# One-hot compares for four tokens at once, scaled on ScalarE, and 48 instead of 72 tiles of U ahead, in a transformer layer with single-neuron experts

## The chip, the cores and the metric

The kernel runs on one core of a Trainium2 chip. The metric is the device time of one execution in microseconds (us), lower is better. TensorE does the matrix products, VectorE and ScalarE work on the elements, GpSimd issues the gathers, and SyncE and ScalarE issue most of the transfers between the chip's memory and the on-chip memory.

## The reference

One layer for 512 latent tokens of width 2048, with 256 tokens of context: a modulated norm, a mixing half (pooling beside differential attention), then a half of experts, then a last norm. The change lies in the experts' half. For every token, two halves of a query score 128 keys each; the best 16 of each side are combined, and the 16 best pairs of eight heads name 128 experts out of 128 x 128, each with a gate. Then

```python
u = peer_u[eidx]                                   # (token, head, 16, 2048)
act = gelu(einsum('thkd,td->thk', u, hb))
v = peer_v[eidx]
out = einsum('thkd,thk->td', v, gate * act)
```

All of it is float32.

## The kernel before

**Two ways for the experts.** The first 128 tokens gather the rows of `peer_u` and `peer_v` that they picked (`slots`): 128 gathers of U and 128 of V, each a row of 2048 per token, each followed by one pass of VectorE (lines 676 and 687). The other 384 tokens (`TD`) take all 16384 experts densely, in 128 tiles of 128 experts: `u_tile` multiplies a tile of U with the tokens and applies the gelu, the result is multiplied with the gates (zero for experts that a token didn't pick), and the products with V sum it up. Float32 factors are split into a high and a low part, a cast on ScalarE and a subtraction on VectorE (`split`, lines 112 and 113; `weights` does it for what comes from memory, with three buffers of each half tile), and three products stand for one. A tile of U has 48 products (line 709).

**Gates.** `decode` makes, from a token's picks, the first key's number, the second key's and the gate; `pick` transposes these into `pT`, so that each token is a column. `combine` then makes the 128 x 128 table of gates of one token as a product of two one-hot matrices: L has a one where the first key's number is the column's, R has the gate where the second key's is. L is one compare on VectorE (line 751), R a compare with a multiplication in the same instruction (line 752), each of 128 x 128, with ten buffers each (`LRB`). Four tokens, a group here, share one buffer of `pg` in PSUM, which ScalarE copies into `ge` (line 754); `pg` has two buffers. After eight groups, 32 tokens, the 2 MB of `ge` go to `g_s` in the chip's memory (line 757); `ge` has one buffer.

**Stages.** The gates need the decoded picks, and V's products need the gates. So 72 tiles of U (`SPILL`) run ahead: their results go to `sg_s` in memory (`spill`). Five tiles (`PRE`) come first, then `combine` is advanced behind each tile until its 96 groups are made, two tiles (`GEND`) before the end:

```python
for n in range(todo):
    spill(1)
    if n in late:
        pick(late[n])
    if n >= GS:
        pump(GRATE)
    while made < 8 * (TD // 32) * (n + 1) / (todo - GEND):
        made += 1
        next(steps, None)
```

`pump` starts the gathers that are due, `GRATE` for a tile. Then come 16 chunks of eight tiles (`CH`) in the order 72 to 127, 0 to 71: for a tile from 72 on U is computed in the chunk, for the others the spilled result is read back (`sg`); then four column blocks of V's products (line 841, 288 products a chunk) with `pump` between them at `RATE`. Seven chunks have U in them, nine do not.

**What sets the order.** The order of instructions on each engine is fixed when the program is built: a scheduler goes through the instructions in program order and lets a later one go first where, by its planned costs, an earlier one would still wait. On the chip each engine takes its instructions in that order, and waits by semaphores.

Of the kernel before, what the change touches and what calls it, by code (L numbers as in the profile page):

```python
# [10 lines left out]
F32 = mybir.dt.float32  # L11
# [4 lines left out]
AF = mybir.ActivationFunctionType  # L16
OP = mybir.AluOpType
# [6 lines left out]
T = 512  # L24
# [7 lines left out]
TOPK = 16  # L32
TD = 384

# the first two sections of the modulation: k-tiles that go to the tensor engine whole (the others
# split in two), the steps after which a block of tokens is normalized, buffers
SEC0 = (3, 7, 11, 15)
SEC1 = (0, 1, 2, 3, 4, 5)
BLK = (0, 2, 3, 5, 7, 9)
AWB = 7  # L40
AHB = 2

# attention, in steps of a projection's k-tile (48 a head): how long the products of zc are held back,
# a head's first block of scores and the next ones (QKL: the last head's), from scores to transposed
# probabilities and on to the values, the operands of the next head's keys, pooling's last product
LEAD = 3
QK0 = 8
QKD = 4
QKL = 6
# [5 lines left out]
ADA_REST = 4  # L55
POOLS = (3, 2, 1, 0)

# experts: tiles of U ahead of V, tiles a chunk, tiles before the gates are combined and the end
# that is left free, when tokens' picks are decoded, rows gathered a tile
SPILL = 72  # L60
CH = 8
PRE = 5
LATE = ((8, 0), (12, 2), (30, 3))
GS = 9
GEND = 2
GRATE = 1.15
LRB = 10
RATE = (256 - (SPILL - PRE - GS) * GRATE) / (2 * NKEY - SPILL - 11)


def body(tc, xin, ctx, vecs, lamv, ada1, ada2, adab2, n2g, fing, win, poolw, wout, wq, keys,
         ut, u, v, rope, icnt, out):
    nc = tc.nc
    V, S, G, E = nc.vector, nc.scalar, nc.gpsimd, nc.tensor

    with ExitStack() as whole:
# [18 lines left out]
        ones = const.tile([128, 1], F32, name="ones")  # L95
        iota = const.tile([128, 128], F32, name="iota")
# [27 lines left out]
            V.tensor_scalar(tmp, ss, 1.0 / n, EPS, op0=OP.mult, op1=OP.add)  # L124
            G.tensor_tensor(dst, tmp, nhalf[:, 0:dst.shape[-1]], OP.pow)

# [1 line left out]
        # h^T without its shift; the shift's columns (latent, context) stand beside it as two  # L128
        # more tokens, and what they project to is added to every token's projection.
        # columns: shifts 0:2, context 2:258, shifts 258:260, latent 260:772  # L130
        hstack = ExitStack()
        hp = pool(hstack, "hp", side="right")
        h_hi = hp.tile([128, KT, HW], F32R, name="h_hi")
# [12 lines left out]
        S.copy(cols, svp[:, 0:89])  # L146
        S.activation(scol.rearrange("p j k -> p (j k)"), cols[:, 0:32], AF.Silu)
        V.tensor_scalar(g08, cols[:, 88:89], 0.8, None, op0=OP.mult)
        # silu(c), silu(c_ctx): whole (beside two columns of zeros), and split in two
        sc4 = a1.tile([128, KT, 4], F32, name="sc4")  # L150
        sr4 = a1.tile([128, KT, 4], F32R, name="sr4")
        V.memset(sc4, 0.0)
        V.tensor_copy(sc4[:, :, 0:2], scol.rearrange("p j k -> p k j"))
        split(sr4[:, :, 0:2], sr4[:, :, 2:4], sc4[:, :, 0:2])

        # normalized tokens, transposed in place: [feature, block, k-tile, token]
        xall = a0.tile([128, 6, D], F32, name="xall")

        def norm_block(b):
# [75 lines left out]
            split(h_hi[:, :, c0:c0 + 2], h_lo[:, :, c0:c0 + 2], sh)  # L235
        a1stack.close()

# [1 line left out]
        with ExitStack() as st:  # L239
            at = pool(st, "at")  # L240
            ps = pool(st, "psA", 1, PSUM)
# [14 lines left out]
                V.tensor_add(dst, dst, zs[:, 0:n])  # L256

            def project(idx, zl, zc):
                # one step a k-tile; zc's first products are held back for LEAD steps
                late = []  # L260
                for half in range(2):
                    hi, lo = weights(win[idx, :, half * 8:(half + 1) * 8, :], [128, 8, 128])
                    for k8 in range(8):
                        k = half * 8 + k8

                        def mm(part, k=k, k8=k8, hi=hi, lo=lo):
                            for p, (x, y) in enumerate(((hi, h_hi), (hi, h_lo), (lo, h_hi))):
                                E.matmul(part[0], x[:, k8, :], y[:, k, part[1]], start=k == 0 and p == 0, stop=k == KT - 1 and p == 2)  # L268
                        mm(zl)
                        late.append(mm)  # L270
                        if k >= LEAD - 1:
                            for m in late:
                                m(zc)
                            late = []
                        if k < KT - 1:
                            yield
# [22 lines left out]
                agenda.setdefault(n, []).append(fn)  # L299

            def k_operands(h):
                # stacked for the products: [k_hi; k_hi] of each map, and k_lo
                d = heads[h]
                kr = d["kr"]
                d["kk"] = kk = at.tile([128, 2, TK], F32R, name="kk")
                d["k_lo"] = k_lo = at.tile([128, TK], F32R, name="k_lo")
                for m, a, b in HALVES:
                    S.copy(kk[a, m, :], kr[a])
                    nc.scalar.dma_start(kk[b, m, :].bitcast(F32), kk[a, m, :].bitcast(F32))
                    V.tensor_sub(k_lo[a], kr[a], kk[a, m, :].bitcast(F32))  # L310
# [121 lines left out]
                    G.dma_start(m_s[:, sec * 512:(sec + 1) * 512], b)  # L432

            def pooling(g):
                # the window's mean minus the token itself
                ic = at.tile([128, T], F32, name="aw", bufs=3)
                nc.scalar.dma_start(ic, icnt[g:g + 1, :].to_broadcast([128, T]))
                zl, zc = psums()
                yield from project(36 + g, (zl[:, 0:256], slice(516, HW)), (zc, slice(258, 516)))
                sb = shift_of(zc)  # L440
                za = at.tile([128, T + 16], F32, name="kr", bufs=2)
                zb = at.tile([128, T + 16], F32, name="aw", bufs=3)
                V.memset(za[:, 0:8], 0.0)
                V.memset(za[:, T + 8:T + 16], 0.0)
                S.activation(za[:, 8:264], zc[:, 2:258], AF.Identity, bias=sb[:, 0:1])
                S.activation(za[:, 264:T + 8], zl[:, 0:256], AF.Identity, bias=sb[:, 0:1])
                n, src, w = T + 16, za, 1
                while w < 2 << g:
                    n -= w
                    V.tensor_add(zb[:, 0:n], src[:, 0:n], src[:, w:w + n])  # L450
                    src, w = zb, 2 * w
                V.tensor_mul(ic, zb[:, 8 - w // 2:8 - w // 2 + T], ic)
                V.tensor_sub(ic, ic, za[:, 8:T + 8])
                pw = at.tile([128, 128], F32, name="on", bufs=2)
                nc.scalar.dma_start(pw, poolw[g])

                def mix():
                    pt = ps.tile([128, T], F32, name="T", bufs=2)
                    E.matmul(pt, pw, ic, start=True, stop=True)
                    yo = at.tile([128, T], F32, name="aacc")  # L460
                    V.tensor_scalar(yo, pt, cols[:, 80 + g:81 + g], cols[:, 84 + g:85 + g], op0=OP.add, op1=OP.mult)
                    G.dma_start(o_s[g], yo)
                at_step(48 * H + 16 * POOLS.index(g) + 16 + MIX, mix)
                yield

            for h in range(H):
# [4 lines left out]
                for qp in range(2):  # L471
                    t = units[4 * qp + 3] + PT0
# [14 lines left out]
            steps, ada, owed_ada, n = fill(), ada_steps(), 0.0, 0  # L487
            while agenda or steps is not None:
                if steps is not None and next(steps, 0) == 0:
                    steps = None  # L490
# [9 lines left out]
        pstack.close()  # L500
        hstack.close()

# [1 line left out]
        f0p = pool(whole, "f0p")  # L504
        f0 = f0p.tile([128, D], F32, name="f0")
        xstack = ExitStack()
# [5 lines left out]
        with ExitStack() as st:  # L512
            op = pool(st, "op", side="right")
# [62 lines left out]
            nc.sync.dma_start(f_lo.bitcast(F32), fq_lo[:, :, 128:T].bitcast(F32))  # L576
        xstack.close()

# [1 line left out]
        ub = pool(whole, "ub")  # L580
        psU = pool(whole, "psU", 1, PSUM)
        rtstack = ExitStack()
# [5 lines left out]
        with ExitStack() as st:  # L588
# [12 lines left out]

            for hp in range(16):
                pq = ps.tile([128, T], F32, name="pq", bufs=2)
                # the first product begins with the tokens that are ready first
                ws = []
                for cs in ((slice(0, 256), slice(256, T)) if hp == 0 else (slice(0, T),)):
                    for half in range(2):
# [52 lines left out]
            V.reciprocal(sm, sm)  # L660
            V.tensor_tensor(g3, g3, sm[:, :, None].to_broadcast([128, PH, 16]), op=OP.mult)

# [1 line left out]
        acc0 = gp.tile([128, D], F32, name="acc0")  # L664
        vw = v.rearrange("(a b) d -> a b d", b=NKEY)

# [54 lines left out]
        with ExitStack() as st:  # L721
# [16 lines left out]
                S.copy(picks[b], pt)  # L738

            def combine():  # L740
                # gates by token and expert: one one-hot product a token
                for tt in range(TD // 32):
                    ge = gb.tile([128, 128, 32], F32, name="ge", bufs=1)
                    pT = picks[1 + tt // 4]
                    for t4 in range(0, 32, 4):
                        pg = ps.tile([128, 4, 128], F32, name="pg", bufs=2)
                        for i in range(4):
                            t = (tt % 4) * 32 + t4 + i
                            L = gb.tile([128, 128], F32, name="L", bufs=LRB)
                            R = gb.tile([128, 128], F32, name="R", bufs=LRB)  # L750
                            V.tensor_scalar(L, iota, pT[:, 0, t:t + 1], None, op0=OP.is_equal)
                            V.tensor_scalar(R, iota, pT[:, 1, t:t + 1], pT[:, 2, t:t + 1], op0=OP.is_equal, op1=OP.mult)
                            E.matmul(pg[:, i, :], L, R, start=True, stop=True)  # L753
                        S.copy(ge[:, :, t4:t4 + 4].rearrange("p b t -> p t b"), pg)
                        if t4 < 28:
                            yield
                    nc.scalar.dma_start(g_s[tt], ge)
                    yield
# [177 lines left out]
```

## Time and profile before

| | |
|---|---|
| median of 3 runs | 3678.8 us (3674.42 to 3694.43) |
| profiled execution, first to last instruction | 3665.6 us; the runs' times hold what lies around the span too, and the median is 13.2 us above it |
| busy: TensorE, VectorE, ScalarE, GpSimd | 3533.5, 2669.5, 1391.0, 463.5 us |
| granted share of TensorE's full clock over the span | 0.991 |
| moved by DMA | 854.44 MB, 233 GB/s |

A busy share is a mean over stages with different limits. A row of the trace names an engine, a line of the kernel, what is written and read, and the time; "idle before" with a releaser says what ended the wait. The profile's times are microseconds from the first instruction.

### The profile page before, as it was taken

How to read it: one execution, taken by the hardware profiler on the slowest of the kernel's cores; microseconds unless marked ns; L12 is line 12 of the kernel's file. 1: busy time of each engine (PE TensorE's matmuls, PEld its weight loads, DVE VectorE, ACT ScalarE, POOL GpSimd, SP SyncE). 2: the span in 40 equal slices, each digit the busy share in tenths (PEclk: the TensorE clock that was granted, in tenths of full speed). 3: DMA queues.
4: the chain of work that ended last, by engine and by line, in shares of the span. 5: the costliest groups of instructions: out<-in, count | busy, mean ns of one | idle time of the engine just before them, and what ended most of it. 6: DMA issues, size and time to landing. Idle time of an engine off the chain costs nothing.

```text
span 3665.6 us, 49666 instructions
## 1 busy us (share of the span) xinstructions
PE 3533.5 (96%) x18938; PEld 3084.7 (84%) x18938; DVE 2669.5 (73%) x4379; ACT 1391.0 (38%) x1975; POOL 463.5 (13%) x390
## 2 busy tenths in 40 slices
PE   7999999999998999999999999999999999999997
PEld 2588888899777889999999978988988977777776
DVE  5787787756537999788778666666666677787776
ACT  7454545455323234344444322323323322232223
POOL 0000000000120000111111112112121111111100
PEclk9999999999999999999999999999999999999998
DMA  9755555422645225688888877777778788888875
GB/s 331 271 171 175 164 176 174 146 66 78 211 147 197 93 97 183 248 332 293 302 287 299 291 251 276 246 268 281 250 273 279 249 306 302 295 301 304 302 237 173
DMA packets 307034, 854.44 MB, mean 233 GB/s; under 512 B 25985, under 2 KB 98394, under 8 KB 270954
## 3 DMA queue, kind: packets, MB, share of 16 engines
q1 hardware_dynamic: 240842, 498.48, 41.8%
q0 software_dynamic: 40992, 283.17, 20.4%
q10 hardware_dynamic: 24960, 69.61, 5.5%
q8 instruction: 148, 2.42, 0.3%
q14 instruction: 92, 0.75, 0.1%
HBM read 788.21 MB, written 51.94 MB: 229 GB/s over the span
## 4 chain that ended last, share of the span: by engine, by line
PE 67%; DMA 10%; issue 10%; DVE 8%; ACT 3%; POOL 2%; ACTq 0%; POOLq 0%; SPq 0%; DVEq 0%
PE pu L709 25%; PE pv L841 15%; PE zl L268 5%; PE pq L614 5%; PE pw L540 5%; DMA aw<-in_ada_dram 4%; PE zc L268 3%; DMA row<-in_v_dram,e 2%; PE pg L753 2%; DVE aacc L425 2%; PE sc L356 1%; DVE wlo L113 1%; PE pt L193 1%; POOL row L674 1%; DMA row<-in_u_dram,e 1%
## 5 line engine op out<-in xcount | busy, mean ns | idle before, releaser
L112 ACT CAST whi<-raw 128x1024 fp32r<-128x1024 f32 x668 | 701.2, 1051 | 1555.4 <-PE pu L709 482.7
L113 DVE TENSOR_TENSOR wlo<-raw,whi 128x1024 fp32r<-128x1024 f32 x668 | 827.3, 1242 | 429.6 <-ACT whi L112 427.4
L709 PE MATMUL pu<-f_hi,whi 128*128 128x384 f32 x2048 | 693.9, 339 | 0.0
L709 PE MATMUL pu<-f_hi,wlo 128*128 128x384 f32 x2048 | 688.4, 336 | 3.0 <-DVE wlo L113 3.0
L709 PE MATMUL pu<-f_lo,whi 128*128 128x384 f32 x2048 | 688.1, 336 | 0.0
L841 PE MATMUL pv<-wlo,a_hi 128*128 128x512 f32 x1536 | 616.4, 401 | 52.6 <-DVE wlo L113 51.1
L841 PE MATMUL pv<-whi,a_lo 128*128 128x512 f32 x1536 | 612.9, 399 | 0.0
L841 PE MATMUL pv<-whi,a_hi 128*128 128x512 f32 x1536 | 612.3, 399 | 0.3 <-ACT whi L112 0.3
L841 PEld LDWEIGHTS pv<-wlo,a_hi 128*128 128x128 f32 x1536 | 292.2, 190 | 134.3 <-DVE wlo L113 64.6
L709 PEld LDWEIGHTS pu<-f_hi,wlo 128*128 128x128 f32 x2048 | 385.0, 188 | 3.3 <-DVE wlo L113 3.3
L709 PEld LDWEIGHTS pu<-f_lo,whi 128*128 128x128 f32 x2048 | 385.3, 188 | 0.3
L709 PEld LDWEIGHTS pu<-f_hi,whi 128*128 128x128 f32 x2048 | 385.3, 188 | 0.3
L841 PEld LDWEIGHTS pv<-whi,a_hi 128*128 128x128 f32 x1536 | 292.0, 190 | 71.5 <-ACT whi L112 0.7
L841 PEld LDWEIGHTS pv<-whi,a_lo 128*128 128x128 f32 x1536 | 292.3, 190 | 69.8
L687 DVE SCALAR_TENSOR_TENSOR acc<-row,w,acc 128x2048 f32<-128x2048 f32 x127 | 297.9, 2346 | 53.9 <-DMA row<-in_v_dram,e 53.6
L676 DVE SCALAR_TENSOR_TENSOR row<-row,f 128x2048 f32<-128x2048 f32 x128 | 292.1, 2285 | 54.2 <-DMA row<-in_u_dram,e 54.1
L674 POOL DMA_INDIRECT row<-in_u_dram,e x128 | 177.3, 1385 | 1189.3 <-DVE row L676 783.0
L682 POOL DMA_INDIRECT row<-in_v_dram,e x128 | 182.4, 1425 | 845.8 <-DVE acc L687 605.8
L268 PE MATMUL zl<-h_hi,whi 128*128 128x512 f32 (+1 forms) x640 | 238.8, 373 | 0.0
L268 PE MATMUL zl<-h_hi,wlo 128*128 128x512 f32 (+1 forms) x640 | 223.4, 349 | 0.0
L268 PE MATMUL zl<-h_lo,whi 128*128 128x512 f32 (+1 forms) x640 | 223.4, 349 | 0.0
L425 DVE SCALAR_TENSOR_TENSOR aacc<-aw,scol,aacc 128x512 f32<-128x512 f32 x240 | 179.4, 748 | 44.0 <-DMA aw<-in_ada_dram 40.3
(237 smaller groups left out, 5187.9 us busy)
## 6 DMA issues: line engine op xcount, KB each, us to landing
raw<-in_v_dram SPq DMA_DIRECT2D x260, 512.0 KB
raw<-in_ut_dram SPq DMA_DIRECT2D x256, 512.0 KB
aw<-in_ada_dram SPq DMA_DIRECT2D x256, 256.0 KB
raw<-in_win_dram SPq DMA_DIRECT2D x80, 512.0 KB
aw<-in_ada_dram SPq DMA_DIRECT2D x64, 512.0 KB
g_s<-ge ACTq DMA_DIRECT2D x12, 2048.0 KB
gt<-g_s SPq DMA_DIRECT2D x32, 768.0 KB
raw<-in_wout_dram SPq DMA_DIRECT2D x40, 512.0 KB
```

The costliest lines, as they stand in the source:

```text
L112: S.copy(dst_hi, src)
L113: V.tensor_sub(dst_lo, src, dst_hi.bitcast(F32))
L268: E.matmul(part[0], x[:, k8, :], y[:, k, part[1]], start=k == 0 and p == 0, stop=k == KT - 1 and p == 2)
L425: V.scalar_tensor_tensor(acc, w, scol[:, 0, k:k + 1], acc, op0=OP.mult, op1=OP.add)
L540: E.matmul(pw[b], x[:, k, bs], y[:, j, :], start=i + j == 0 and p == 0, stop=i + j == KT - 1 and p == 2)
L614: E.matmul(pq[:, cs], a[:, k8, :], b[:, k, cs], start=k == 0 and p == 0, stop=k == KT - 1 and p == 2)
L674: G.indirect_dma_start(out=row, out_offset=None, in_=u, in_offset=bass.IndirectOffsetOnAxis(ap=e0[:, j:j + 1], axis=0))
L676: tc.keep_in_program_order(V.scalar_tensor_tensor(row, row, 1.0, f0, op0=OP.mult, op1=OP.mult, accum_out=s0[:, j:j + 1]))
L682: G.indirect_dma_start(out=row, out_offset=None, in_=v, in_offset=bass.IndirectOffsetOnAxis(ap=e0[:, j:j + 1], axis=0))
L687: tc.keep_in_program_order(V.scalar_tensor_tensor(acc0, row, w0[:, j:j + 1], acc0, op0=OP.mult, op1=OP.add))
L709: E.matmul(pu, a[:, k8, :], b[:, k, :], start=k == 0 and p == 0, stop=k == KT - 1 and p == 2)
L841: E.matmul(pv[b], x[:, bs], y[:, j, :], start=n + j == 0 and p == 0, stop=n + j == CH - 1 and p == 2)
```

## The change

The two compares are made for four tokens in one instruction each, on 128 x 4 x 128 elements with both operands broadcast; the gate is no longer multiplied in, but follows as a copy with a scale by partition on ScalarE, one per token, in place. L and R have three buffers of four tokens each. `SPILL` is 48, so 80 tiles of U are computed in the chunks (ten chunks with U, six without); `LATE` decodes the third and the fourth block of tokens after tiles 10 and 20; `RATE` follows from `SPILL`. Elsewhere the diff takes out comments alone.

```diff
-SPILL = 72
+SPILL = 48
 CH = 8
 PRE = 5
-LATE = ((8, 0), (12, 2), (30, 3))
+LATE = ((8, 0), (10, 2), (20, 3))
 GS = 9
 GEND = 2
 GRATE = 1.15
-LRB = 10
 RATE = (256 - (SPILL - PRE - GS) * GRATE) / (2 * NKEY - SPILL - 11)
...
                     for t4 in range(0, 32, 4):
                         pg = ps.tile([128, 4, 128], F32, name="pg", bufs=2)
+                        t = (tt % 4) * 32 + t4
+                        L = gb.tile([128, 4, 128], F32, name="L", bufs=3)
+                        R = gb.tile([128, 4, 128], F32, name="R", bufs=3)
+                        for x, side in ((L, 0), (R, 1)):
+                            V.tensor_tensor(x, iota[:, None, :].to_broadcast([128, 4, 128]),
+                                            pT[:, side, t:t + 4, None].to_broadcast([128, 4, 128]), op=OP.is_equal)
                         for i in range(4):
-                            t = (tt % 4) * 32 + t4 + i
-                            L = gb.tile([128, 128], F32, name="L", bufs=LRB)
-                            R = gb.tile([128, 128], F32, name="R", bufs=LRB)
-                            V.tensor_scalar(L, iota, pT[:, 0, t:t + 1], None, op0=OP.is_equal)
-                            V.tensor_scalar(R, iota, pT[:, 1, t:t + 1], pT[:, 2, t:t + 1], op0=OP.is_equal, op1=OP.mult)
-                            E.matmul(pg[:, i, :], L, R, start=True, stop=True)
+                            S.activation(R[:, i, :], R[:, i, :], AF.Copy, scale=pT[:, 2, t + i:t + i + 1])
+                            E.matmul(pg[:, i, :], L[:, i, :], R[:, i, :], start=True, stop=True)
                         S.copy(ge[:, :, t4:t4 + 4].rearrange("p b t -> p t b"), pg)
```

## Rows read from the trace of the kernel before

**Rows 1.** The head of the page: the span and the instructions of the profiled execution.

```profile
span 3665.6 us, 49666 instructions
```

**Rows 2.** Busy time by stretch: from and to, length in us, then for TensorE's matmuls (PE), its weight loads (PEld), VectorE (DVE), ScalarE (ACT) and GpSimd (POOL) the busy us and, in brackets, the instructions; the granted share of TensorE's full clock; the DMA engines' busy share; GB/s. The three stretches are the run-ahead stage with its gates, six chunks with tiles of U in them, and seven without.

```profile
1391.00:2019.40 628.40, 627.93 (x3895) 627.44 (x3895) 514.56 (x1055) 263.48 (x302) 89.03 (x67) 1.00 0.78 280
2102.70:2939.30 836.60, 813.81 (x4034) 729.91 (x4034) 559.39 (x523) 245.75 (x292) 158.13 (x105) 0.99 0.76 264
3011.50:3496.40 484.90, 473.31 (x2017) 377.64 (x2016) 373.57 (x404) 144.05 (x170) 75.66 (x61) 1.00 0.87 300
```

**Rows 3.** The chain of work that ended last, early in the run-ahead stage: start us, us, what, and how many instructions in a row.

```profile
1391.10 8.34 PE pu L709 x48
1399.43 1.78 PE pg L753 x16
...
1409.55 0.89 PE pg L753 x8
```

**Rows 4.** Who waited for whom from 1344 to 2022 us: us in total, times, the longest.

```profile
ACT ge L754 <- DMA g_s<-ge: 37.9, 10, 7.0
...
PE pu L709 <- DVE wlo L113: 3.0, 1, 3.0
...
PE pg L753 <- ACT ge L754: 0.5, 1, 0.5
```

**Rows 5.** The chain again, where a chunk with tiles of U runs without a wait: its next eight tiles of U, then its products with V.

```profile
2598.14 66.56 PE pu L709 x384
2664.70 67.19 PE pv L841 x288
```

**Rows 6.** Who waited for whom from 2022 to 2950 us, as in rows 4.

```profile
DVE row L676 <- DMA row<-in_u_dram,e: 40.0, 16, 5.2
...
PE pv L841 <- DVE wlo L113: 22.8, 8, 5.4
```

**Rows 7.** Busy time by stretch, as in rows 2, around one of those waits.

```profile
2124.00:2129.00 5.00, 0.94 (x5) 0.41 (x3) 4.40 (x6) 1.04 (x1) 0.94 (x1) 0.96 0.67 241
2129.00:2136.00 7.00, 6.11 (x15) 4.83 (x16) 5.32 (x5) 0.00 (x0) 1.68 (x1) 0.54 0.86 291
```

**Rows 8.** VectorE in order of time, two tokens' first compares: start us, us, line, operation, out<-in.

```profile
1599.68 0.28 DVE L751 TENSOR_SCALAR L<-iota,pT 128x128 f32<-128x128 f32 x1
...
1600.14 0.28 DVE L751 TENSOR_SCALAR L<-iota,pT 128x128 f32<-128x128 f32 x1
```

**Rows 9.** Groups of instructions on VectorE over the whole span, forms kept apart: line, operation, out<-in, shapes, count | busy us, mean ns of one | idle us before them and what ended it.

```profile
L113 DVE TENSOR_TENSOR wlo<-raw,whi 128x1024 fp32r<-128x1024 f32 x668 | 827.3, 1242 | 429.6 <-ACT whi L112 427.4 <-PE pu L709 1.0
...
L687 DVE SCALAR_TENSOR_TENSOR acc<-row,w,acc 128x2048 f32<-128x2048 f32 x127 | 297.9, 2346 | 53.9 <-DMA row<-in_v_dram,e 53.6
...
L752 DVE TENSOR_SCALAR R<-iota,pT 128x128 f32<-128x128 f32 x384 | 131.5, 343 | 0.0
...
L751 DVE TENSOR_SCALAR L<-iota,pT 128x128 f32<-128x128 f32 x384 | 109.7, 286 | 22.4 <-PE pg L753 22.1
...
L650 DVE TENSOR_TENSOR eq<-pf,iota 128x1024 f32<-128x1024 f32 x16 | 19.0, 1220 | 0.0
...
L787 DVE TENSOR_TENSOR acc<-acc,g 128x512 f32<-128x512 f32 x16 | 10.5, 683 | 0.0
```

**Rows 10.** The same on ScalarE.

```profile
L112 ACT CAST whi<-raw 128x1024 fp32r<-128x1024 f32 x668 | 701.2, 1051 | 1555.4 <-PE pu L709 482.7 <-PE pv L841 367.1 <-DMA raw<-in_v_dram 242.0
...
L754 ACT COPY ge<-pg 128x512 f32<-128x512 f32 x96 | 102.8, 1139 | 38.4 <-DMA g_s<-ge 37.9 <-PE pg L753 0.4
...
L711 ACT ACTIVATE sg<-pu 128x384 f32<-128x384 f32 x128 | 62.4, 488 | 27.7 <-PE pu L709 27.6
...
L214 ACT ACTIVATE h_hi<-xall,gs 128x512 fp32r<-128x512 f32 x16 | 11.3, 708 | 2.3 <-DVE gs L208 2.3
...
L214 ACT ACTIVATE h_hi<-xall,gs 128x256 fp32r<-128x256 f32 x16 | 7.9, 493 | 0.0
```

**Rows 11.** TensorE's matmuls in order of time; in square brackets the idle time before and what ended it.

```profile
1565.18 1.16 PE L753 MATMUL pg<-R,L 128*128 128x128 f32 x8 [0.47 <-ACT ge L754]
```

**Rows 12.** ScalarE and its queue (ACTq) in order of time at three places: from the issue of a transfer to `g_s` to the next gate copy.

```profile
1547.71 0.33 ACTq L757 DMA_DIRECT2D g_s<-ge  x1
...
1564.06 1.95 ACT L754 COPY ge<-pg 128x512 f32<-128x512 f32 x2 [1.37 <-DMA g_s<-ge]
...
1758.07 1.05 ACT L112 CAST whi<-raw 128x1024 fp32r<-128x1024 f32 x1 [3.11 <-PE pu L709]
...
1760.55 0.35 ACTq L757 DMA_DIRECT2D g_s<-ge  x1
...
1768.18 1.05 ACT L112 CAST whi<-raw 128x1024 fp32r<-128x1024 f32 x1 [3.11 <-PE pu L709]
1772.49 1.12 ACT L754 COPY ge<-pg 128x512 f32<-128x512 f32 x1 [3.26 <-DMA g_s<-ge]
1773.39 0.54 ACT L711 ACTIVATE sg<-pu 128x384 f32<-128x384 f32 x1
...
1866.42 0.33 ACTq L757 DMA_DIRECT2D g_s<-ge  x1
...
1875.02 1.12 ACT L754 COPY ge<-pg 128x512 f32<-128x512 f32 x1
```

**Rows 13.** Who waited for whom from 2950 us to the end, as in rows 4.

```profile
DVE sg L823 <- DMA sg<-sg_s: 69.6, 27, 6.9
```

## The prediction

> **What bounds the kernel now.** I read the page first, then cut the expert part into stages with the table of windows, then read who waits for whom in each stage, and last the rows of the operations that the change touches.
>
> The span is 3665.6 us [rows 1], 13.2 us under the median of the runs, 3678.8. I make the sum against the span and add 13.2 at the end. A difference of 0.5% (18 us) is about what a measurement of this kernel can tell from no change.
>
> In the stage that runs U ahead and combines the gates (1391 to 2019 us), TensorE is busy 627.93 of 628.40 us; VectorE has 82% and ScalarE 42% [rows 2]. The chain there is nothing but matmuls: a tile of U takes 8.33 us, the products of four tokens 0.89 us, those of eight 1.78 us [rows 3]. From 1344 us on, TensorE waits 3.5 us in all [rows 4]. So this stage is TensorE's: time comes off it by taking products away, and it gets longer only where TensorE is made to wait.
>
> In the second stage, a mixed chunk (eight tiles of U, then eight of V) costs 66.56 + 67.19 = 133.75 us when nothing waits [rows 5]. The window of six such chunks is 836.6 us against 802.5, so 5.7 us are lost in each. Seven chunks of V alone take 484.9 us against 470.4: 2.1 us lost in each [rows 2]. The losses are matmuls that wait for the low half of V's weights, behind VectorE, which itself waits for gathered rows [rows 6]; after such a wait of 5 us the granted clock falls to 0.54 over the next 7 us, a stretch at the lower of its two levels, 1.2 GHz [rows 7].
>
> **The change part by part.**
>
> *Tiles moved.* TensorE's products stay the same: 24 tiles of U leave the run-ahead stage (24 x 8.33 = 200 us) and come back in the second, where three chunks of V alone become mixed (3 x 66.56 = 200 us). Their 24 spills and reloads of 192 KB go; nothing in the run-ahead stage waits for a spill. What differs is the loss: three mixed chunks for three others cost 3 x (5.7 - 2.1) = 11 us. Bounds: -34 us if the waits for gathered rows were to go, +25 us if the added chunks each lose what the worst do (about 8.5 us, a 5 us wait and its half clock). I take +11. The gathers' rates hardly move: 1.15 a tile ahead, then 216.9/197 = 1.101 a step where it was 189.3/173 = 1.094.
>
> *VectorE's compares.* Now a token's two compares take 0.45 us from start to start [rows 8], 1.82 us for four tokens. The new ones are two one-result compares of 128x512. The trace has none of this shape; a compare of two broadcast operands over 128x1024 took 1.22 us and a two-operand multiply of 128x512 0.68 us [rows 9]. So 2 x 0.68 = 1.37 us; bounds 1.2 (starts overlap by some 0.08 us each, as those of [rows 8]) and 2.4 (the price of 1024 elements, if 512 cost as much). Over 96 groups VectorE saves 43 us. TensorE doesn't wait for it in this stage beyond 3 us [rows 4], so I count nothing. VectorE has to do its work in a shorter stage: 43 tiles x 8.33 + 96 x 0.89 = 444 us hold 86 weight subtractions (107 us), 192 compares (131), 39 gathered rows (92) and some two decodings (twelve passes of 1024 elements each, 30), 360 us or 81% by [rows 9], about the share of now. If that cover went, its lack would come straight on to TensorE.
>
> *ScalarE's scaling.* 384 new copies of 128x128 with a scale by partition. Two such copies stand in the trace: 0.708 us for 512 and 0.493 us for 256 elements, so 0.215 us for 256 and 0.386 us for 128 [rows 10]. I take 0.386 (148 us); bounds 0.29 (a copy behind another starts some 0.1 us before that one's end, or more: 1772.49 and 1773.39 in [rows 12]) and 0.49 (the price of 256). In the 444 us ScalarE then has 86 casts (90), 43 gelus (21), 96 gate copies (103) and 148: 362 us, 82% instead of 42% [rows 2, 10]. That is below the whole, but ScalarE works in order. Behind a waiting instruction stand the casts of U's weights, which have about 8 us in hand (two half tiles are ready ahead), the gelu, the scalings and the gate copies, for which TensorE waits with two buffers of `pg` only.
>
> *The wait that moves up.* `ge` has one buffer: after eight groups 2 MB go to `g_s`, and the first gate copy of the next 32 tokens has to wait for the landing. With one group a tile and a half that cost ScalarE 37.9 us and TensorE once 0.5 us [rows 4]; the one place [rows 11] shows the mechanism: products of a third group wait for a buffer of `pg` that the blocked gate copy still holds. Landings: 12 us in the middle case (1760.55 to 1772.49), 16.4 in the worst, 8.6 or less in the best [rows 12]. Now count. Groups made after tile n are 96(n+1)/41 rounded up: 3, 5, 8, 10, 12, 15, 17 and so on, two or three behind each tile. Where the eighth group is the first of its batch, its copy ends and the transfer is issued 2.5 us after the tile's matmuls (1758.0 to 1760.55). The batch's second product ends at 1.8, the next tile at 10.1, its first group at 11.0, and there the third group wants its buffer. That comes free at 2.5 + 12.5 + 1.1 (the gate copy) = 16.1 us. The engines' order, fixed beforehand, expects the landing sooner: it has the gate copy before the gelu of 1768.2 [rows 12], so under some 8.7 us. If it puts other matmuls in front for that long, TensorE waits the rest, 12.5 - 8.5 = 4 us; in program order it would be 5. Of the eleven borders, those after groups 32, 40, 48, 56, 72 and 88 fall so that the third group comes this early and gathers run beside it (they start with tile 9, group 22); after 16 there are no gathers yet; after 8, 24, 64 and 80 the third group comes a tile later, at 20 us, and nothing waits. So 6 x 4 = 24 us, and each with a stretch of lower clock: a 5 us gap was followed by 0.54 over 7 us, that is 3.2 us more [rows 7], of which I take 1.7 for a 4 us gap: 10 us. Together +34, bounds 0 (landings of 8.6 us) and 6 x (7.8 + 3.2) = 66 us (landings of 16.4).
>
> The rows have the 2 MB land in 12 to 16 us where gathers and U's weights run beside them [rows 12], with the DMA engines 0.78 busy in this stage [rows 2]. The Trainium skill, DMA: Bandwidth & Descriptors, Specifications, gives a core some 358 GB/s of HBM; as an estimate by it, 2 MB alone would land in 6 us, all the borders would be hidden, and the sum would be +11 instead of +45. Its section Issuing engines are not separate DMA queues says why that price isn't to be had here: transfers of all queues share the same 16 engines. The rows agree with the second, and I go by them.
>
> *Three groups in a batch* (some 14 tiles): the third wants a `pg` buffer about 0.9 us before the first copy has ended. I count nothing, since matmuls of the next tile can stand there; 13 us at most. *Decodings* after tiles 10 and 20 instead of 12 and 30: nothing, with the two decodings' 30 us in VectorE's 81% above.
>
> **Sum.** 0 (products) + 11 (mixed chunks) + 34 (borders) = +45 us: span 3711, time 3724.
>
> **The rivals.**
>
> *Hidden (same).* The landings are as quick as in the best row, or the third groups come later in TensorE's order than I think; only the chunks count: 0 to +17 us, about 3690. For it: ScalarE has idle time left, and the present stage hides eleven such waits but for 0.5 us, and one landing of 8.6 us is there [rows 12]. Against: the third group now comes 11 us after the batch instead of two tiles or more.
>
> *Faster.* The mixed chunks lose by waits for gathered rows. If these come of how gathers and U's matmuls happen to fall together, they may be gone with another grouping: four waits of 5 us, each with 3.2 us of lower clock, make -33 us; and V's chunks wait less for reloaded tiles (69.6 us of VectorE, 27 waits [rows 13]) with a third of them gone. It decides if the borders cost under 15 us at the same time: about 3650. For it: the DMA share is 0.76 in mixed chunks and 0.87 in the others [rows 2]. Against: the waits came with that lower share.
>
> *ScalarE becomes the bound.* At 0.49 us a scaling it has 402 us, and with eleven blocked waits of 4 us 446 of 444 us: then casts come late too, and the stage grows by 60 to 90 us, about 3750 to 3780.
>
> **How the numbers follow.** My forecast, slower by 20 to 62 us (3699 to 3741), has 0.43; hidden 0.28; faster 0.17; ScalarE the bound 0.12. So faster by over 0.5% 0.17, within 0.5% 0.28, slower 0.55. The likeliest is 3724 us. The range leaves out about half of the faster and half of the ScalarE case: 3655 to 3765 us; the likeliest one's own is 3699 to 3741.
>
> **What would show it.** In the run-ahead stage: TensorE's wait for ScalarE's gate copy at about six borders, 4 us each, with a lower clock behind it; two compares of 0.68 us for four tokens; scalings of 0.39 us; ScalarE near 82%. In the second: ten mixed chunks at 139 us. I am wrong if the stage stays at 100% of TensorE (hidden), or if the casts of U's weights are what TensorE waits for (ScalarE).

## The result: 3730 us, 1.3% slower, by waits at the borders

| | before | after |
|---|---|---|
| median of the runs | 3679.38 us (3674.42 to 3694.43, 4 runs) | 3730.06 us (3721.96 to 3738.08, 4 runs) |
| profiled execution, span | 3665.6 us | 3736.3 us |
| ratio | | 1.0133 (95%: 1.0110 to 1.0157) |

Predicted were 3724 us. The profiled execution of after took 3738.08 us, the longest of its four. That of before lies under the shortest of its four: with the same 1.8 us around its span it would be 3667.4. So the spans differ by 70.7 us where the medians differ by 50.7. Sizes below are taken from the spans where places are meant, and from the medians where times are compared. Two executions of the experiments, of 4953.2 and 4414.1 us at a granted clock of 0.654 and 0.735, are in no median below.

The head of after's page, to set beside [rows 1] and the table of before (TensorE, VectorE, ScalarE, GpSimd: busy us, share, instructions):

```profile
span 3736.3 us, 49438 instructions
...
PE 3561.5 (95%) x18938; PEld 3105.3 (83%) x18938; DVE 2615.2 (70%) x3803; ACT 1498.6 (40%) x2359; POOL 466.8 (12%) x390
```

ScalarE has 108 us more than before, VectorE 54 us less, TensorE the same instructions.

Busy time by stretch of the kernel before, columns as in [rows 2]: from the first tile after the first transposed picks to the first product with V, and from there to the last.

```profile
1390.60:2102.70 712.10, 711.63 (x4378) 711.13 (x4377) 565.93 (x1107) 292.61 (x339) 104.52 (x76) 1.00 0.79 282
2102.70:3652.30 1549.60, 1496.70 (x6913) 1273.31 (x6912) 1102.66 (x1125) 460.44 (x560) 257.26 (x183) 0.99 0.78 270
```

The same two stretches of after, then its nine whole mixed chunks and five chunks of V alone:

```profile
1399.50:1969.10 569.60, 531.07 (x3228) 524.34 (x3226) 388.45 (x442) 339.61 (x650) 66.50 (x48) 0.97 0.71 248
1969.10:3723.30 1754.20, 1700.24 (x8065) 1475.13 (x8064) 1225.11 (x1214) 520.84 (x634) 298.89 (x211) 0.98 0.78 267
1969.10:3223.20 1254.10, 1220.16 (x6049) 1093.64 (x6049) 841.02 (x783) 368.40 (x437) 232.86 (x159) 0.99 0.77 265
3223.20:3571.70 348.50, 339.99 (x1441) 271.00 (x1441) 267.75 (x282) 102.57 (x123) 57.50 (x46) 1.00 0.89 303
```

By the pace of [rows 3], the first stretch of before is 75 tiles of U and 96 groups, 75 x 8.33 + 96 x 0.89 = 710.2 us: 1.9 us are lost. That of after is 51 tiles and 96 groups, 510.3 us: 59.3 us are lost, with a mean granted share of 0.97. The second stretch should have grown by three times 66.56, 199.7 us, and grew by 204.6. So the time went where it was forecast, in the run-ahead stage. The rest of the 70.7 us, 8.9, lies ahead of both stretches (1390.6 against 1399.5), in code that the change doesn't touch; I take it as scatter, since in the experiments' traces this point lies anywhere from 1390.5 to 1398.7. The two stretches together grew by 62.1 us, 11 more than the medians did, so a size read from two spans can be off by that much.

Who waited in after's run-ahead stage (us, times, longest), the rows that answer to [rows 4]:

```profile
ACT ge L755 <- DMA g_s<-ge: 62.2, 10, 9.5
...
PE pg L754 <- ACT ge L755: 31.4, 18, 5.9
...
PE pg L754 <- ACT R L753: 5.4, 2, 3.3
```

TensorE waited 36.8 us for the gates' groups (31.4 + 5.4), where it was 0.5 us. Two borders show the two ways in which it came. ScalarE after the eighth group, in order of time:

```profile
1434.74 0.33 ACTq L758 DMA_DIRECT2D g_s<-ge  x1
...
1442.12 0.39 ACT L753 ACTIVATE R<-R,pT 128x128 f32<-128x128 f32 x1
...
1446.33 1.01 ACT L755 COPY ge<-pg 128x512 f32<-128x512 f32 x1 [3.82 <-DMA g_s<-ge]
1447.15 0.39 ACT L753 ACTIVATE R<-R,pT 128x128 f32<-128x128 f32 x1
```

and TensorE there:

```profile
1447.59 0.49 PE L754 MATMUL pg<-R,L 128*128 128x128 f32 x2 [3.28 <-ACT R L753]
```

The second group after the border has its fourth scaling (1447.15) in ScalarE's order behind the gate copy that waits for the landing (1446.33); TensorE has done the products of three tokens and six of the next tile's, and stands 3.28 us before the fourth's. The other way, after group 40, is the one that the prediction counted on. ScalarE:

```profile
1594.14 0.33 ACTq L758 DMA_DIRECT2D g_s<-ge  x1
...
1605.29 1.89 ACT L755 COPY ge<-pg 128x512 f32<-128x512 f32 x2 [4.88 <-DMA g_s<-ge]
```

TensorE:

```profile
1606.35 0.79 PE L754 MATMUL pg<-R,L 128*128 128x128 f32 x2 [4.45 <-ACT ge L755]
```

Here the products of the third group wait for the buffer of `pg`, 4.45 us. Stretches around it, columns as in [rows 2]:

```profile
1601.50:1606.30 4.80, 0.40 (x3) 0.08 (x1) 1.52 (x3) 1.01 (x2) 0.00 (x0) 0.87 0.79 326
1606.30:1611.80 5.50, 5.45 (x20) 5.45 (x21) 2.06 (x3) 4.62 (x11) 0.00 (x0) 0.50 0.01 3
```

After the wait the granted share is 0.50, the lower of the clock's two levels, 1.2 GHz, for the whole of the next 5.5 us. That answers to [rows 7].

TensorE's waits at the other borders, in order of time: after groups 16, 32, 48, 56, 64, 72, 80 and 88. After group 24 there is none.

```profile
1491.52 1.16 PE L754 MATMUL pg<-R,L 128*128 128x128 f32 x8 [1.33 <-ACT ge L755]
...
1568.79 1.96 PE L754 MATMUL pg<-R,L 128*128 128x128 f32 x12 [3.14 <-ACT ge L755]
...
1652.95 3.36 PE L754 MATMUL pg<-R,L 128*128 128x128 f32 x14 [2.30 <-ACT ge L755]
...
1691.97 0.94 PE L754 MATMUL pg<-R,L 128*128 128x128 f32 x6 [3.48 <-ACT ge L755]
...
1727.91 1.22 PE L754 MATMUL pg<-R,L 128*128 128x128 f32 x4 [2.12 <-ACT R L753]
...
1776.44 2.07 PE L754 MATMUL pg<-R,L 128*128 128x128 f32 x8 [5.87 <-ACT ge L755]
...
1825.99 1.27 PE L754 MATMUL pg<-R,L 128*128 128x128 f32 x8 [2.15 <-ACT ge L755]
...
1860.82 2.77 PE L754 MATMUL pg<-R,L 128*128 128x128 f32 x12 [3.53 <-ACT ge L755]
```

The new operations, columns as in [rows 9]:

```profile
L753 ACT ACTIVATE R<-R,pT 128x128 f32<-128x128 f32 x384 | 121.5, 395 | 19.8 <-DVE R L750 19.1 <-ACT R L753 0.5
...
L750 DVE TENSOR_TENSOR L<-iota,pT 128x512 f32<-128x512 f32 x96 | 65.9, 687 | 82.5 <-PE pg L754 82.4
L750 DVE TENSOR_TENSOR R<-iota,pT 128x512 f32<-128x512 f32 x96 | 65.7, 685 | 0.0
```

### The profile page after: what moved, and what is told of

Its sections match the earlier page's. It is cut to its first block, busy times and chain, and to the rows that moved or that the text cites. A ratio compares the mean times of both kernels' runs of the same rounds, so it can differ in the third digit from the quotient of the medians.

```text
span 3736.3 us, 49438 instructions
## 1 busy us (share of the span) xinstructions
PE 3561.5 (95%) x18938; PEld 3105.3 (83%) x18938; DVE 2615.2 (70%) x3803; ACT 1498.6 (40%) x2359; POOL 466.8 (12%) x390
## 4 chain that ended last, share of the span: by engine, by line
PE 53%; issue 17%; DMA 15%; DVE 9%; ACT 3%; POOL 3%; SPq 0%; POOLq 0%; DVEq 0%; ACTq 0%
PE pu L708 15%; PE pv L842 14%; PE zl L267 5%; PE pq L613 5%; PE pw L539 5%; DMA aw<-in_ada_dram 4%; DMA row<-in_v_dram,e 4%; PE zc L267 3%; POOL row L673 2%; DMA sg<-sg_s 2%; DVE wlo L112 2%; DMA g_s<-ge 2%; DVE aacc L424 2%; DMA raw<-in_v_dram 1%; DMA row<-in_u_dram,e 1%
```

## The experiments

For the first four kernels the stretches are given, cut as above, and the loss of the first against 710.2 us (72 tiles ahead) or 510.3 us (48). The kernel before ran beside each group: its medians were 3677.3, 3676.1, 3677.05 and 3674.6 us.

**The compares alone.** The kernel after, with the old numbers of tiles and times:

```diff
-SPILL = 48
+SPILL = 72
-LATE = ((8, 0), (10, 2), (20, 3))
+LATE = ((8, 0), (12, 2), (30, 3))
```

> The four-token compares and ScalarE's scaling, with 72 tiles ahead and the old times of decoding. Theory B (borders: the time goes where the next 32 tokens' first gate copy waits for the transfer of ge, because groups come closer together): groups are 1.5 a tile again, the third group comes two tiles after the border, so nearly nothing waits: 3676 to 3695 us, TensorE's waits in the run-ahead stage under 8 us. Theory S (the 384 scalings themselves hold ScalarE up): about 3730 us as in the changed kernel, since they are all here. Theory C (the three chunks that become mixed cost it): 3679 us, as before.

Measured: 3681.09 us (3672.2 to 3691.64, 10 runs), ratio 1.0014 (0.9994 to 1.0034): no difference to before. The run-ahead stretch, and TensorE's wait for a scaling in it:

```profile
1392.70:2111.30 718.60, 714.45 (x4378) 711.80 (x4377) 507.87 (x531) 403.59 (x723) 117.85 (x76) 1.00 0.79 280
```

```profile
PE pg L754 <- ACT R L753: 0.8, 2, 0.6
```

8.4 us are lost, 0.8 of them in a wait for a scaling and none for a gate copy. All 384 scalings are there; ScalarE's work by itself costs next to nothing at this pace, so theory S falls. Theories B and C named the same time here and aren't told apart by it.

**The tiles alone.** The kernel before, with 48 tiles ahead and the new `LATE`:

```diff
-SPILL = 72
+SPILL = 48
-LATE = ((8, 0), (12, 2), (30, 3))
+LATE = ((8, 0), (10, 2), (20, 3))
```

> 48 tiles ahead and the new times of decoding, with the old compares (two results per token on VectorE, no scaling on ScalarE). Theory B: the waits for a buffer of pg behind the blocked gate copy remain (31.4 of the 36.9 us that TensorE waits in the changed kernel), those for a scaling behind that copy go: 3710 to 3735 us. Theory S: the scalings are gone, so 3680 to 3690 us. Theory C: as the changed kernel, about 3730 us, but with no waits in the run-ahead stage. VectorE has some 404 of 444 us to do in that stage, so waits for U's low halves may appear beside.

Measured: 3709.08 us (3702.08 to 3714.03), ratio 1.0101 (1.0080 to 1.0123), a little under what theory B named. The new `LATE` wasn't run by itself; no wait of TensorE for a decoding stands in the traces. Both stretches, and TensorE's wait for the gate copy:

```profile
1395.10:1944.30 549.20, 525.62 (x3227) 519.85 (x3226) 446.45 (x1018) 232.47 (x267) 62.16 (x48) 0.98 0.74 258
1944.30:3686.40 1742.10, 1694.60 (x8064) 1471.94 (x8063) 1223.99 (x1213) 521.03 (x633) 301.87 (x211) 0.99 0.77 269
```

```profile
PE pg L753 <- ACT ge L754: 22.1, 16, 5.3
```

The run-ahead stretch loses 38.9 us with no scaling in the kernel: that is the buffer of `pg` alone, behind the blocked copy, and its low clock. The second stretch is 1742.1 us, less than 1549.6 + 199.7, so theory C, which put the time there, falls.

**Two buffers of `ge`.** The kernel after, with

```diff
-ge = gb.tile([128, 128, 32], F32, name="ge", bufs=1)
+ge = gb.tile([128, 128, 32], F32, name="ge", bufs=2)
```

> The changed kernel with two buffers of ge, so that the next gate copy has no landing to wait for. Theory B: the 62 us of ScalarE and the 37 us of TensorE at the borders go, with the low clock behind them: 3680 to 3695 us, what is left is the three mixed chunks (5 to 11 us). Theory S: 3725 to 3730 us. Theory C: 3725 to 3730 us.

Measured: 3684.79 us (3678.46 to 3690.36, 10 runs), ratio 1.0028 (1.0013 to 1.0043). It lies 7.5 us above the kernel before beside it, where the change lay 50.7 above: 43 us are gone with the wait for the landing.

```profile
1395.50:1918.20 522.70, 516.29 (x3227) 511.07 (x3226) 387.29 (x442) 340.17 (x650) 77.93 (x48) 1.00 0.76 271
1918.20:3663.00 1744.80, 1697.70 (x8065) 1473.30 (x8063) 1223.40 (x1213) 521.28 (x633) 298.32 (x211) 0.99 0.77 269
```

```profile
PE pg L754 <- ACT ge L755: 4.7, 10, 0.9
```

No gate copy waits for a landing any more. TensorE still waits ten times, up to 0.9 us, for a gate copy: the third group of a batch. The run-ahead stretch loses 12.4 us at a granted share of 1.00. All 384 scalings are in this short stage too, so theory S falls here as well.

**Four buffers of `pg`.** The kernel after, with

```diff
-pg = ps.tile([128, 4, 128], F32, name="pg", bufs=2)
+pg = ps.tile([128, 4, 128], F32, name="pg", bufs=4)
```

> The changed kernel with four buffers of pg instead of two, one buffer of ge. Theory B, with the buffer of pg as the link to TensorE: the third and fourth groups no longer need the blocked copy's buffer, 31.4 us of waits go with their low clock, 5.4 us for scalings stay: 3685 to 3705 us. Theory B, with the scalings behind the blocked copy as the link: the waits turn into waits for scalings and the time stays at 3715 to 3730 us. Theories S and C: 3725 to 3730 us.

Measured: 3708.64 us (3705.79 to 3716.39, 3 runs), ratio 1.0092 (1.0065 to 1.0119), between the ranges of the two forms of theory B and in neither; the profiled execution is the longest of the three.

```profile
1398.00:1951.80 553.80, 525.68 (x3228) 522.84 (x3227) 388.24 (x442) 340.04 (x650) 67.95 (x48) 0.97 0.72 256
1951.80:3701.60 1749.80, 1699.16 (x8065) 1474.18 (x8063) 1224.71 (x1214) 521.50 (x634) 296.97 (x211) 0.99 0.77 268
```

```profile
PE pg L754 <- ACT R L753: 27.0, 7, 6.0
```

The waits for a gate copy are gone, and 27.0 us of waits for a scaling stand in their place (5.4 in after). 43.5 us are lost. So there are two links from the blocked copy to TensorE; taking away either leaves 31 to 32 of the 51 us (3708.64 here, 3709.08 without the scalings, both against 3677.3), and only the landing's wait itself is worth removing.

**Mixed chunks from the other side.** The kernel before with `SPILL = 96`.

> The kernel before with 96 tiles ahead: four mixed chunks instead of seven, gates spread over 91 tiles. It tests the +11 us for three more mixed chunks from the other side. If a mixed chunk loses 3.6 us more than one of V alone, as I worked out: 3666 to 3672 us. If, as the four runs before this one suggest, the second stage loses the same whatever the mix: 3675 to 3682 us.

Measured: 3663.01 us, ratio 0.9964 (0.9951 to 0.9977): 13 us faster, a little under the first range, and the reading that the mix doesn't matter fails on this side. Three whole mixed chunks, and the stretch from the last tile of U to the last product with V:

```profile
2314.40:2731.80 417.40, 406.07 (x2019) 364.09 (x2018) 279.30 (x261) 123.01 (x147) 73.98 (x52) 0.99 0.75 263
2731.80:3648.20 916.40, 887.80 (x3744) 708.91 (x3743) 702.49 (x776) 276.73 (x341) 136.40 (x104) 0.99 0.84 284
```

The three lose 417.4 - 3 x 133.75 = 16.2 us, 5.4 each. More tiles ahead also mean more rows gathered ahead: by the kernel's rates some 162 gathers are left for the second stage instead of 189. None of the runs that raise `SPILL` tells fewer mixed chunks from fewer gathers there.

**Gathers moved to U's part.** The kernel before, with

```diff
-                        pump(RATE)
+                        pump(1.35 * RATE)
...
-                        pump(0.5 * RATE)
+                        pump((0.325 if ibs[0] >= SPILL else 0.5) * RATE)
```

> The kernel before with 1.35 times as many gathers started beside the tiles of U in mixed chunks and 0.65 times as many beside their products with V; the sum is the same. If the 5 us waits at the start of V's products come from gathered rows that are late beside V's weights (DMA share 0.82 there, 0.67 beside U): most of the 34 us lost in six mixed chunks goes, 3645 to 3662 us. If they come from anything else, such as V's weights themselves or the gathers left over for later: 3675 to 3690 us.

Measured: 3682.46 us, ratio 1.0019 (1.0005 to 1.0033): no gain. TensorE's waits from 2022 to 2950 us, beside [rows 6]:

```profile
PE pv L841 <- DVE wlo L113: 15.9, 11, 2.7
PE pu L709 <- DVE wlo L113: 6.6, 3, 2.9
```

```profile
DVE row L676 <- DMA row<-in_u_dram,e: 67.7, 27, 4.9
```

V's products wait 15.9 us instead of 22.8, but now U's wait 6.6, and VectorE waits 67.7 us for rows where it was 40.0. The waits were split and moved, not removed. By stretch, first this run's six mixed chunks and what follows them, then what follows them in before:

```profile
2107.60:2935.10 827.50, 808.76 (x4033) 725.49 (x4032) 560.63 (x522) 243.82 (x292) 153.70 (x105) 1.00 0.76 266
2935.10:3656.50 721.40, 687.84 (x2881) 545.85 (x2880) 539.79 (x601) 214.42 (x268) 94.11 (x77) 0.98 0.81 273
```

```profile
2939.30:3652.30 713.00, 682.89 (x2881) 543.40 (x2879) 543.27 (x602) 214.68 (x268) 99.13 (x78) 0.99 0.82 278
```

The six chunks lose 827.5 - 802.5 = 25.0 us instead of 34.1; the ten blocks of V's products behind them, 671.9 us without a wait, lose 49.5 instead of 41.1.

**Both.** 96 tiles ahead and the moved gathers:

> Both edits, 96 tiles ahead and the gathers shifted in the four mixed chunks that are left. If the late rows cost the mixed chunks their time: 3650 to 3665 us, with little left to gain from having fewer of them. If not: 3675 to 3685 us.

Measured: 3653.51 us, ratio 0.9946 (0.9926 to 0.9967), 9.5 us under 96 tiles alone. The first range was wide enough to hold 96 tiles alone as well, so the run doesn't decide between the two. Where the 9.5 us come from isn't shown: the profiled executions differ by 11.0 us, of which 8.2 lie ahead of the run-ahead stage (1390.5 against 1398.7), where the edit changes nothing, and 4.3 in the second stretch.

**The kernel after with two buffers of `ge` and the moved gathers.**

> The changed kernel with two buffers of ge and the shifted gathers, ten mixed chunks. If the late rows cost the mixed chunks their time, ten of them gain more than seven do: 3630 to 3650 us, under the kernel before by 1%. If not: 3680 to 3690 us, as with two buffers of ge alone.

Measured: 3684.93 us, ratio 1.0032 (1.0018 to 1.0046): as without the move.

**A slower pace of gathers in the second stage.** The kernel before with `SPILL = 96` and `GRATE = 1.3`, so that more rows are gathered in the run-ahead stage:

> The kernel before with 96 tiles ahead and 1.3 instead of 1.15 gathers a tile in the run-ahead stage, so 1.00 instead of 1.085 a step in the second. The second stage of the kernel with 96 tiles still loses 59 us to waits, the run-ahead stage 6. If the second stage's waits come from gathered rows that its faster pace makes late: 3640 to 3655 us. If they come whatever the pace: 3658 to 3668 us, as with 96 tiles alone. If the run-ahead stage can't take the faster pace, over 3670 us.

Measured: 3649.62 us, ratio 0.9935 (0.9919 to 0.9951), in the first range. The trace bears the reason out only in part: of the 13.7 us between the profiled executions with and without the edit, 5.6 lie in the second stretch, 4.7 in the run-ahead stretch, the rest ahead of both. With `SPILL = 112`:

> As the run before, with 112 tiles ahead: two mixed chunks, rate 0.96 in the second stage. If each mixed chunk costs 3.6 us more than one of V alone: 7 us under the run before, 3633 to 3650 us. If the mix doesn't matter: the same as the run before.

Measured: 3637.24 us (3633.85 to 3644.17), ratio 0.9894 (0.9876 to 0.9911), the fastest of all, 1.1% under the kernel before and in the first range; the rows left for the second stage fell with it, from some 149 to 129. With the moved gathers at 96 tiles:

> 96 tiles ahead, 1.3 gathers a tile ahead, and the gathers shifted to U's part in the four mixed chunks. If slower pace and shift each take waits away: 3635 to 3650 us. If the shift only moves waits from V's products to U's: as 96 tiles with 1.3 alone, within 5 us.

Measured: 3642.42 us (3634.9 to 3658.29, 5 runs), ratio 0.9917 (0.9895 to 0.9939). It lies 7.2 us under the same kernel without the move, whose runs went from 3644.53 to 3657.87; the two ranges overlap too far to decide. With `SPILL = 128`, no mixed chunk left:

> All 128 tiles of U ahead, 1.3 gathers a tile there, no mixed chunk left; rate 0.92 in the second stage. If a mixed chunk costs about 4 us more than one of V alone, two fewer of them: 3625 to 3636 us. If chunks of V alone now lose as much, since all their tiles are read back: 3636 to 3650 us.

Measured: 3644.54 us, ratio 0.9916 (0.9901 to 0.9931): no further gain. It lies in the second range, but not for the reason given there. The sixteen chunks of V alone take 1101.6 us, of which 26.6 are lost, less than in any other run. What takes the gain away, by the trace, is the first product with V, which stands for factors made from read-back results, with no tile of U left to do meanwhile:

```profile
2525.15 0.79 PE L841 MATMUL pv<-whi,a_hi 128*128 128x512 f32 x1 [16.73 <-ACT a_hi L112]
```

What the fastest one takes away is the wait of V's products for their low halves over the whole span, first in the kernel before,

```profile
PE pv L841 <- DVE wlo L113: 51.1, 24, 5.4
```

then with 112 tiles ahead:

```profile
PE pv L841 <- DVE wlo L113: 23.4, 12, 5.1
```

## Why the prediction was right, and where its terms were off

**Direction and place: right.** The run-ahead stage was TensorE's in before, and it is the borders that took it out of TensorE's hands. With a second buffer of `ge`, 43 us go, where the forecast for the borders was 34; 7.5 us stay, where it was 11 for the mixed chunks. That the sum came within 6 us of the median is in part luck: the two terms are off in opposite directions.

**The borders: right mechanism, mis-sized beside it.** I counted six borders of eleven, those where the third group comes early, at 4 us and 1.7 us of low clock each. Those six (after groups 32, 40, 48, 56, 72 and 88) have waits of 22.8 us in all, 3.8 each, where I had 24. What I missed lies around them. After groups 8, 16, 64 and 80, where I counted nothing, TensorE waits 8.9 us in all, and ten more waits of 0.3 to 1.5 us at third groups away from the borders make 5.2. The link that I left out is the scalings', which caused the waits after 8 and 64: I named them among what stands behind a blocked ScalarE, but counted only the buffers of `pg`. The low clock was also too small in my sum: of the 59.3 us lost, 38.5 are idle time (569.6 - 531.07) and 20.8 are longer products; with two buffers of `ge` the products were longer by 6.0 at a granted share of 1.00, so some 15 us, an estimate, belong to the low clock, where I had 10. The kernel with the old compares has the buffer of `pg` alone and loses 37 us more than before in its run-ahead stretch, close to my 34; with the scalings the loss is 57. The landings were quicker than the 12.5 us I took: 11.6 us after group 8 (1434.74 to 1446.33), 11.2 after group 40 (1594.14 to 1605.29), and 9.5 to 14.0 over the ten that a gate copy waited for. They stay well above the 6 us that I had estimated from the Trainium skill (DMA: Bandwidth & Descriptors, Specifications) for 2 MB alone, which no run here shows. Its section Issuing engines are not separate DMA queues has all transfers on the same 16 engines; the trace agrees, with the engines 0.71 busy in this stretch.

**The matmuls put in front: right.** Behind the border after group 8 TensorE does six products of the next tile before it stands, behind the one after group 40 three.

**The groups in threes: right within its bound.** Nothing was counted, 13 us at most; 4.7 us show with two buffers of `ge`, and 5.2 in after.

**The three mixed chunks, +11 us: one price right, the other wrong.** The loss per mixed chunk was read rightly. The nine whole ones of after lose 1254.1 - 9 x 133.75 = 50.4 us, 5.6 each, so they take 139 us as forecast; with 96 tiles three lose 5.4 each. The step that failed is the other side of the difference: 2.1 us for a chunk of V alone, from a window that left out the first and the last two of them. From the last tile of U to the last product with V, seven blocks of V's products in after and in the kernel with the old compares took:

```profile
3223.20:3723.30 500.10, 480.08 (x2017) 381.49 (x2016) 384.08 (x431) 152.44 (x197) 66.04 (x53) 0.98 0.82 272
```

```profile
3194.90:3686.40 491.50, 476.88 (x2016) 380.58 (x2016) 382.90 (x430) 152.81 (x196) 66.39 (x52) 0.99 0.81 277
```

Against 7 x 67.19 = 470.3 us they lose 29.8 and 21.2; before's ten blocks lose 41.1. So the three that went had cost 4 to 7 us each, about as much as the mixed chunks that came. That is why the second stretch is only 5 us longer than the moved tiles explain in after, 7 and 5 us shorter in the kernels with the old compares and with two buffers of `ge`, and the same with four of `pg`. On the other side, thirteen such blocks with 96 tiles lose 916.4 - 873.5 = 42.9 us, hardly more than ten, so there three mixed chunks fewer gave 16 us in the second stretch, and the time fell by 13. Why three more blocks of V cost nothing and three fewer gave 11 to 20 us stays open.

**Prices: right.** The compares of 128x512 took 0.686 us (0.68 taken), the scalings 0.395 us (0.386). ScalarE was busy 340 of 570 us in a stretch of 51 tiles, where I had worked out 362 of 444 for 43: starts overlap (384 scalings of 0.395 us fill 121.5 us), which I had left to the lower bound. It was never the bound, as the compares alone and two buffers of `ge` show. VectorE saved 54 us of busy time; 43 were worked out.

**The base.** I added 13.2 us to the span for what lies around it. The run of 3738.08 us has a span of 3736.3, so 1.8 us lie around it; the rest was the distance of that execution from the median. As both sides of the difference have it, the sum of +45 us was hardly touched.

**The rivals.** "Hidden" is what a second buffer of `ge` makes of the change (3685 us, I had 3690). "ScalarE the bound" fell with the compares alone, and "faster" with the second stretch: V's products still wait for their low halves there. Moving the gathers brought nothing to the kernel before (3682.46 us) or to the changed one with two buffers of `ge` (3684.93); with 96 tiles ahead it gave 9.5 us, for a cause that isn't shown.

## What to carry to other kernels

Before work is packed into a shorter stage, count the waits that come once per so many steps: a single buffer that a slow transfer empties is hidden as long as the steps after it are further apart than the landing, and shows at each border when they are not. Look at everything that stands in order behind the blocked instruction, not only at the buffer that it holds: with two links, removing one left most of the waits to the other, and a second buffer at the root removed both. An average over a window that leaves out the first and last chunks isn't the price of one more.

## What the runs showed of the hardware that was not expected

Short waits of TensorE were followed by the lower clock: after 3.28 us (1447.59) and 4.45 us (1606.35) the next products took 0.52 us instead of 0.34. Seven such stretches fell into after's run-ahead stage, 31 us at the lower level in all, behind waits of 2.1 to 5.9 us. But after waits of 3.14 us (1568.79) and 3.48 us (1691.97) the products kept their 0.34, so the length of the last wait alone doesn't tell what follows. And gathered rows are late when more of them are started beside U's tiles too (67.7 us of VectorE's waits against 40.0), although the DMA engines are less busy there: 0.67 against 0.82 beside V's products, in one mixed chunk of before (2178.6 to 2312.2 us).
